# A hybrid decoder block in fp32: every second transposed-form weight unit takes its low halves from adding DMAs issued by GpSimd

## The chip, the core and the metric

The kernel runs on one core of a Trainium2 chip. The metric is the device time of one execution in microseconds (us). Two executions of the kernel before took 1184.29 and 1184.67 us, median 1184.48 us. The profile shown below is one further execution of the same program; its span, from its first to its last instruction, is 1182.7 us.

The engines are named as the profile names them: PE is the matrix engine (PEld its weight loads), DVE the vector engine, ACT the scalar engine, POOL is GpSimd, SP the engine that here only issues DMAs. A "q" behind an engine's name is its instruction queue.

## The reference, cut to what matters

One decoder layer on 256 tokens of width 2048, everything in float32:

```python
h = rms_norm(x, g_pre[l])
proj = h @ w_in[l]                      # 2048 x 17,936, split into 14 parts
y_a = pool_mixer(a_val, a_gate, ...)    # causal pooling, width 1024
y_b = swa_mixer(sq, sk, sv, s_gate)     # windowed attention, 12 heads of 128
y_c = gla_mixer(cq, ck, cv, c_lr, c_gate, ...)   # gated linear attention, 4 heads
y_m = mem_attn(mq, m_gate, mem, ...)    # attention into 256 memory tokens
gates = jax.nn.sigmoid(g_logits + b_merge[l])
merged = sum of gates[b] * (y_b @ w_br_b)        # four branches
x = x + rms_norm(merged @ w_out[l], g_post[l])
```

Nearly all of the arithmetic is in the products with the weights, which are read once each; the DMAs move 230 MB in all.

## The kernel before, in words

**Split products.** A float32 product is made from rounded halves. Every weight tile `raw` is split into `hi`, which is `raw` rounded to the matrix engine's reduced format (fp32r), and `lo = raw - hi`, rounded likewise; the activations are split in the same way. A product is then hi·hi + hi·lo + lo·hi. `split_w` (L110 to L115) does it for weights, up to 1024 columns at a time: L113 is the rounding copy on ACT, L114 the subtraction on DVE. Such a piece of 128 x 1024 is called a half here, since two of them make one loaded unit of 128 x 2048 (1 MB).

**Two forms of a product.** `a_block` (L117) keeps the activations stationary and streams the weights. `b_unit` (L146) is the transposed form: the weights are stationary and the activations stream. One unit makes 128 output columns for all 256 tokens: 16 k-steps, each one matmul with `hi` against both halves of the activations (512 columns, L156) and one with `lo` against their high half (256 columns, L157). There are 72 such units: the queries and keys of the window attention (`sq`, `sk`, 24 units, names such as `sk01` for head 0, group 1), its gate (`sg`, 4), the memory keys (`km`, 4), the memory queries and gates (`mq`, `mg`, 8), the linear attention's queries and keys (`cq`, `ck`, 8) and gate (`cg`, 8), the pooling values and gates (`av`, `ag`, 16). Everything else goes through `a_block`: the values, the merge gates (`g...`), the branch projections (`b...`) and the output (`o0` to `o4`).

**Buffers.** A unit is loaded by SP (`load_raw`, L107) into one of 3 `raw` buffers. There are 5 `hi` and 5 `lo` buffers, each for one half. So the split of a half can begin when the matmuls that read the half five places earlier are done, four halves before its own turn on PE. An SP load waits until the `raw` buffer is free again, and the loads behind it wait with it.

**After a unit**, ACT copies the second half of the accumulator out (`...s`, L161), DVE adds the first half to it (L162) and scales it; a gate also goes through a tanh on ACT (L306).

**Background work.** The attention heads, the linear attention and the pooling are generators in a queue. `pull(1)` (L68) runs one step of the first generator; `b_unit` calls it between its two halves (L159) and at its end (L164), `a_block` after every or every second half. Each step's instructions stand in the engines' streams at that point, with one `yield` between what is made and what uses it.

**Order.** Each engine runs its own instructions strictly in the order in which the built program has them. That order is set when the program is built, and differs in places from the order of the code. An instruction that waits holds up all that stand behind it on its engine.

Of the kernel before, what the change touches and what calls it, by code (L numbers as in the profile page):

```python
# [9 lines left out]
R = mybir.dt.float32r  # L10
AF = mybir.ActivationFunctionType
ALU = mybir.AluOpType
AX = mybir.AxisListType

P = 128
# [14 lines left out]
NB_HILO = 5  # L30
# [7 lines left out]
def kernel(ctx, tc, ins, out):  # L38
    nc = tc.nc
    ten, vec, act, pool, sync = nc.tensor, nc.vector, nc.scalar, nc.gpsimd, nc.sync  # L40

    cst = ctx.enter_context(tc.tile_pool(name="cst", bufs=1))
    wp = ctx.enter_context(tc.tile_pool(name="wp", bufs=1))
# [15 lines left out]
    def acc(name, shape):  # L59
        return ps.tile(shape, F32, tag="acc", bufs=4, name=name)  # L60
# [1 line left out]
    def tiny(name, shape, bufs=4):  # L62
        return big.tile(shape, F32, tag="tiny", bufs=bufs, name=name)

# [1 line left out]
    queue = []  # L66

    def pull(n):  # L68
        while n > 0 and queue:
            try:  # L70
                next(queue[0][1])
                n -= 1
            except StopIteration:
                queue.pop(0)
# [5 lines left out]
            except StopIteration:  # L80
                queue.pop(0)

# [1 line left out]
    vecs = cst.tile([P, 52], F32, name="vecs")  # L84
    act.dma_start(vecs[:], ins["vecs"])
    ones = cst.tile([P, P], F32, name="ones")
# [11 lines left out]
    half = cst.tile([P, 2], F32, name="half")  # L98
    pool.memset(half[:], -0.5)

# [1 line left out]
    raw_count = [0]  # L102

    def load_raw(src, n):
        raw = wp.tile([P, 2048], F32, tag="raw", bufs=NB_RAW, name=f"raw{raw_count[0]}")
        raw_count[0] += 1
        sync.dma_start(raw[:, :n], src[:, :n])  # L107
        return raw

    def split_w(raw_ap, n, name):  # L110
        hi = wp.tile([P, 1024], R, tag="hi", bufs=NB_HILO, name=name + "h")
        lo = wp.tile([P, 1024], R, tag="lo", bufs=NB_HILO, name=name + "l")
        act.activation(hi[:, :n], raw_ap, AF.Copy)  # L113
        vec.tensor_tensor(lo[:, :n], raw_ap, hi[:, :n].bitcast(F32), op=ALU.subtract)  # L114
        return hi, lo  # L115

    def a_block(name, units, stat, nw, evac, load=None, per_split=None):  # L117
        """out[token, column]: activations stationary, weights moving."""
        accs = [acc(f"{name}a{t}", [P, 512]) for t in range(2)]
        nk = 4 * len(units)  # L120
        for u, src in enumerate(units):
            raw = load_raw(src, 4 * nw) if load is None else load(u, src)
            nk_s = max(1, 1024 // nw) if per_split is None else per_split(u)
            for hf in range(4 // nk_s):
                hi, lo = split_w(raw[:, hf * nk_s * nw : (hf + 1) * nk_s * nw], nk_s * nw, f"{name}{u}{hf}")
                for kk in range(nk_s):
                    k = 4 * u + nk_s * hf + kk
                    ws = slice(kk * nw, (kk + 1) * nw)
                    for t in range(2):
                        sh, sl = stat(k)  # L130
                        ts = slice(t * P, (t + 1) * P)
                        o = accs[t][:, :nw]
                        ten.matmul(o, lhsT=sh[:, ts], rhs=hi[:, ws], start=(k == 0), stop=False)  # L133
                        ten.matmul(o, lhsT=sh[:, ts], rhs=lo[:, ws], start=False, stop=False)  # L134
                        ten.matmul(o, lhsT=sl[:, ts], rhs=hi[:, ws], start=False, stop=(k == nk - 1))  # L135
                if hf % 2 == 0:
                    pull(1)
            pull(1)

        def finish():  # L140
            for t in range(2):
                evac(t, accs[t][:, :nw])

        return finish

    def b_unit(name, src, mov, evac):  # L146
        """out[column, token]: weights stationary, activations moving."""
        a = acc(f"{name}a", [P, 512])
        raw = load_raw(src, 2048)
        for hf in range(2):  # L150
            hi, lo = split_w(raw[:, hf * 1024 : (hf + 1) * 1024], 1024, f"{name}{hf}")
            for kk in range(8):
                k = 8 * hf + kk
                ws = slice(kk * P, (kk + 1) * P)
                mh, _ = mov(k)
                ten.matmul(a[:], lhsT=hi[:, ws], rhs=mov.both(k), start=(k == 0), stop=False)  # L156
                ten.matmul(a[:, :T], lhsT=lo[:, ws], rhs=mh, start=False, stop=(k == KT - 1))  # L157
            if hf == 0:
                pull(1)  # L159
        both = c2(f"{name}s", [P, T])  # L160
        act.activation(both[:], a[:, T:], AF.Copy)  # L161
        vec.tensor_tensor(both[:], a[:, :T], both[:], op=ALU.add)  # L162
        evac(both[:])
        pull(1)  # L164

# [1 line left out]
    def make_T(name, srcT, g):  # L167
        hl = [e8(f"{name}hl{i}", [P, 4, 2, T], R) for i in range(4)]

# [25 lines left out]
        return chunk, at  # L195

    def make_rstd(name, src):
        """1/rms of each token: a column per token tile, and along the free axis for all partitions."""
        ssq = cst.tile([P, 2, 2], F32, name=f"{name}ssq")
        mean = cst.tile([P, 2], F32, name=f"{name}mean")  # L200
        col = cst.tile([P, 2], F32, name=f"{name}col")
        row = cst.tile([P, T], F32, name=f"{name}row")

        def gen():
            for t in range(2):
                for c in range(2):
                    xt = c4(f"{name}x{t}{c}", [P, D // 2])
                    sync.dma_start(xt[:], src[t][:, c * (D // 2) : (c + 1) * (D // 2)])
                    act.activation(xt[:], xt[:], AF.Square, accum_out=ssq[:, t, c : c + 1])
                    yield  # L210
            vec.tensor_tensor(mean[:], ssq[:, :, 0], ssq[:, :, 1], op=ALU.add)
            vec.tensor_scalar(mean[:], mean[:], 1.0 / D, EPS, op0=ALU.mult, op1=ALU.add)
            pool.tensor_tensor(col[:], mean[:], half[:], op=ALU.pow)
            yield
            pr = sm(f"{name}pr", [P, T])
            dg = c2(f"{name}dg", [P, T])
            for t in range(2):
                vec.tensor_scalar(
                    dg[:, t * P : (t + 1) * P], ident[:], col[:, t : t + 1], None, op0=ALU.mult
                )  # L220
            yield
            yield
            ten.matmul(pr[:], lhsT=ones[:], rhs=dg[:], start=True, stop=True)
            vec.tensor_copy(row[:], pr[:])
            yield

        return col, row, gen
# [7 lines left out]
        for _ in gen:  # L235
            pass

    # ================= window attention: values =================
    sv = [c4(f"sv{g}", [P, 2, 512]) for g in range(3)]

    def sv_evac(j):
# [42 lines left out]
    queue.append(("memprep", mem_prep()))  # L284
    a_block("sv2", [ins["w_sv"][2, u] for u in range(4)], h_at, 512, sv_evac(2))()

    # constants that the branches need later
    big_cst = cst.tile([P, 1344], F32, name="big_cst")
    sync.dma_start(big_cst[:], ins["consts"])
    dist0 = big_cst[:, 0:384].rearrange("p (g j) -> p g j", g=3)  # L290
# [6 lines left out]
    vec.tensor_scalar(p_scale, p_scale, 0.5, None, op0=ALU.mult)  # L297

    def silu2_evac(dst):
        """2 * silu of the normalised product."""  # L300

        def evac(a):
            xg = c2("xg", [P, T])
            vec.tensor_tensor(xg[:], a, row[:], op=ALU.mult)  # L304
            th = c2("th", [P, T])
            act.activation(th[:], xg[:], AF.Tanh, scale=0.5)  # L306
            vec.scalar_tensor_tensor(dst, th[:], 1.0, xg[:], op0=ALU.add, op1=ALU.mult)

        return evac
# [11 lines left out]
        act.activation(hi, full, AF.Copy)  # L321
        vec.tensor_tensor(lo, full, hi.bitcast(F32), op=ALU.subtract)  # L322

    # ================= window attention =================
    yb = e8("yb", [P, 2, 4, T], R)
    sgate = c4("sgate", [P, 4, T])

# [53 lines left out]
        queue.append(("swa", swa_head(hh, q3, k3)))  # L381
    drain("memprep")

    # ================= attention into the memory =================
    ym = e8("ym", [P, 2, 4, T], R)
    km = c4("km", [P, 4, T])
    mq = c4("mq", [P, 4, T])
# [43 lines left out]
        b_unit(f"mg{h}", ins["w_mg"][h], h_at, silu2_evac(mgate[:, h, :]))  # L431
        queue.append(("mem", mem_head(h)))

    # ================= gates and branch projections =================
    merged = [e8(f"merged{t}", [P, D]) for t in range(2)]
    started = [False] * 4

# [27 lines left out]

    merge("swa", 1, lambda k: (yb[:, 0, k, :], yb[:, 1, k, :]), 4)

    # ================= gated linear attention =================
    gq = c4("gq", [P, 4, T])
    gk = c4("gk", [P, 4, T])  # L470
    cv = e8("cv", [P, 2, 1024])
# [14 lines left out]
    def gla():  # L486
# [11 lines left out]
        z = c4("z", [P, 4, T])  # L498
        for hp in range(2):
            pz = sm(f"pz{hp}", [P, 2, T])  # L500
            for i in range(2):
                h = 2 * hp + i
                ten.matmul(pz[:, i, :], lhsT=walpha[:, h * P : (h + 1) * P], rhs=lrT[:], start=True, stop=True)
            for i in range(2):
                h = 2 * hp + i
                vec.tensor_scalar(z[:, h, :], pz[:, i, :], b_alpha[:, h : h + 1], None, op0=ALU.add)
        yield
        # log_sigmoid(z) = min(z, 0) - log(1 + exp(-|z|))
        e = c4("e", [P, 4, T])
        act.activation(e[:], z[:], AF.Abs)  # L510
        act.activation(e[:], e[:], AF.Exp, scale=-1.0)
# [26 lines left out]
        for h in range(4):  # L538
# [61 lines left out]
            for vt in range(2):  # L600
                f = 2 * h + vt
# [13 lines left out]
    for j in range(3):  # L615
        c0, n = CV_BLOCKS[j]
# [4 lines left out]

    merge("mem", 3, lambda k: (ym[:, 0, k, :], ym[:, 1, k, :]), 4)

    # ================= causal pooling =================
    PAD = 16
    ya = [e8(f"ya{i}", [P, 8, T], R) for i in range(2)]
    agate = {}
# [78 lines left out]

    merge("pool", 0, lambda k: (ya[0][:, k, :], ya[1][:, k, :]), 8, after=transpose_block)

    # ================= output projection, norm, residual =================
    gpost = e8("gpost", [P, D])  # L710
    xres = [e8(f"xres{t}", [P, D]) for t in range(2)]
    yg = [e8(f"yg{t}", [P, D]) for t in range(2)]
# [28 lines left out]
    for u in range(4):  # L741
        raw = load_raw(ins["w_last"][1, u], 1024)
        last.append(split_w(raw[:, :1024], 1024, f"o4{u}"))
    for t in range(2):
        ts = slice(t * P, (t + 1) * P)
        a = acc(f"o4a{t}", [P, 512])[:, :256]
        for k in range(KT):
            hi, lo = last[k // 4]
# [16 lines left out]
def _layout(x, mem, g_pre, g_post, g_mem, w_in, b_merge, w_pool, pool_scale, w_alpha, b_alpha,  # L765
# [47 lines left out]
    }  # L813
    for j, (c0, n) in enumerate(CV_BLOCKS):
        d[f"w_cv{j}"] = units_a(np.ascontiguousarray(cvlr[:, c0 : c0 + n]), n)[0]
    # constants of the shapes: distances to the keys that each window sees, masks, counts
    i = np.arange(T)[:, None]
    j = np.arange(T)[None, :]
    dist = []
# [5 lines left out]
    a, b = np.arange(P)[:, None], np.arange(P)[None, :]  # L825
# [23 lines left out]
```

## Time and profile before

| | before |
|---|---|
| device time, median of 2 | 1184.48 us (1184.29 to 1184.67) |
| profiled execution, span | 1182.7 us |
| median less span | 1.8 us |
| PE busy | 1172.6 us, 99% |
| DVE busy | 715.9 us, 61% |
| ACT busy | 555.3 us, 47% |
| POOL busy | 13.8 us, 1% (36 instructions) |
| DMA moved | 230.44 MB, mean 195 GB/s |
| granted PE clock | 0.998 |

How to read it. The device time is a little longer than the span because it holds what lies before the first and after the last instruction. A row of grouped instructions gives the line of the kernel, the engine, the operation, what is written and read, the count, the busy time with the mean of one in ns, and the idle time before them with what ended it. A row of one tile gives minimum, median and maximum duration in ns and the first and last start in us. A row of the timeline gives start and duration in us. A row of the stretches gives the stretch, its length, the busy time of each engine with instruction counts, the granted clock, the mean busy share of the 16 DMA engines and GB/s. A row of the DMA issues gives the size of one and the median time from issue to landing.

### The profile page before, as it was taken

The numbers are of one execution on the slowest core, as the hardware profiler recorded it, in microseconds if no ns is written. First come the engines' busy times: TensorE is split into PE (matmuls) and PEld (weight loads), VectorE is DVE, ScalarE is ACT, GpSimd is POOL, SyncE is SP. The second block draws the span as 40 slices with busy tenths as digits, with TensorE's granted clock in tenths as the row PEclk, the third lists the DMA queues.
The fourth block names the chain that finished last, engine by engine and source line by source line (L and its number), as shares of the span: only waits on it lengthen the run. The fifth ranks groups of instructions, "written<-read, shape, count | busy, mean of one in ns | idle before, by whom it ended". The sixth has DMA issues, their size and how long they took to land.

```text
span 1182.7 us, 15065 instructions
## 1 busy us (share of the span) xinstructions
PE 1172.6 (99%) x6014; PEld 1001.8 (85%) x6014; DVE 715.9 (61%) x943; ACT 555.3 (47%) x734; POOL 13.8 (1%) x36
## 2 busy tenths in 40 slices
PE   9999999999999999999999999999999999999997
PEld 7888888888888888899888888888888888888887
DVE  6656665664665555545856666777655555656454
ACT  7656444444554444345644444454444444444441
POOL 0000000000000000000000000000000000000000
PEclk9999999999999999999999999999999999999999
DMA  9867544544445555356444455555555555556642
GB/s 354 324 226 260 178 147 175 178 148 174 178 169 192 200 199 201 133 185 221 178 163 176 156 184 199 179 186 194 214 193 205 204 189 205 193 187 241 257 145 105
DMA packets 38838, 230.44 MB, mean 195 GB/s; under 512 B 4448, under 2 KB 4832, under 8 KB 14832
## 3 DMA queue, kind: packets, MB, share of 16 engines
q1 hardware_dynamic: 38048, 228.28, 54.5%
q10 hardware_dynamic: 720, 1.21, 0.3%
q8 instruction: 47, 0.77, 0.3%
q14 instruction: 23, 0.19, 0.0%
HBM read 227.37 MB, written 2.10 MB: 194 GB/s over the span
## 4 chain that ended last, share of the span: by engine, by line
PE 98%; issue 0%; DMA 0%; DVE 0%; ACT 0%; SPq 0%; DVEq 0%; POOLq 0%; POOL 0%
PE sp L341 1%; PE gmem0a L133 1%; PE gmem2a L133 1%; PE gmem1a L133 1%; PE gswa0a L135 1%; PE gmem2a L135 1%; PE gswa0a L133 1%; PE gmem0a L135 1%; PE gmem1a L135 1%; PE vma L135 1%; PE gmem2a L134 1%; PE gmem0a L134 1%; PE gpool1a L135 1%; PE o0a L135 1%; PE gmem1a L134 1%; PE vma L133 1%
## 5 line engine op out<-in xcount | busy, mean ns | idle before, releaser
L306 ACT ACTIVATE th<-xg 128x256 f32<-128x256 f32 x24 | 9.9, 411 | 18.1 <-DVE xg L304 18.1
L344 DVE SCALAR_TENSOR_TENSOR s<-big_cst,sp 128x128 f32<-128x128 f32 (+1 forms) x24 | 7.3, 349 | 3.5 <-PE sp L341 3.5
L341 PE MATMUL sp<-k,q 128*128 128x128 f32 (+1 forms) x48 | 9.1, 326 | 0.0
L349 ACT ACTIVATE s<-s,st 128x384 f32<-128x384 f32 (+1 forms) x8 | 6.2, 775 | 4.8 <-DVE st L348 4.8
L341 PEld LDWEIGHTS sp<-k,q 128*128 128x128 f32 x48 | 7.3, 190 | 0.8
L578 POOL TENSOR_TENSOR sq<-sq 128x256 f32<-128x256 f32 x4 | 3.4, 854 | 384.5 <-ACT sq L577 360.4
L179 ACT ACTIVATE xhl<-xr,vecs 128x256 fp32r<-128x256 f32 x16 | 6.9, 499 | 1.9 <-DMA xr<-in_xT 1.2
L704 ACT ACTIVATE mTh<-mtp 128x512 fp32r<-128x512 f32 x8 | 4.3, 596 | 6.5 <-PE mtp L702 6.5
L180 DVE SCALAR_TENSOR_TENSOR xhl<-xr,vecs,xhl 128x256 fp32r<-128x256 f32 x16 | 6.8, 482 | 0.7 <-ACT xhl L179 0.6
L367 PE MATMUL po<-pt,sv 128*128 128x256 f32 x24 | 7.2, 380 | 0.0
L179 ACT ACTIVATE mhl<-mr,vecs 128x256 fp32r<-128x256 f32 x16 | 7.0, 495 | 0.0
L180 DVE SCALAR_TENSOR_TENSOR mhl<-mr,vecs,mhl 128x256 fp32r<-128x256 f32 x16 | 6.9, 479 | 0.0
L759 DVE SCALAR_TENSOR_TENSOR yg<-yg,opart,xres 128x640 f32<-128x640 f32 (+2 forms) x8 | 5.5, 748 | 1.3 <-POOL opart L756 1.3
L348 DVE TENSOR_REDUCE st<-s 128x1 f32<-128x384 f32 (+1 forms) x8 | 6.0, 748 | 0.1
L726 ACT ACTIVATE oj<-o4a 128x256 f32<-128x256 f32 x2 | 0.8, 383 | 10.6 <-PE o4a L753 10.6
L362 ACT ACTIVATE pt<-tp 128x384 f32<-128x384 f32 x12 | 5.7, 477 | 0.0
L705 DVE SCALAR_TENSOR_TENSOR mTl<-mtp,mTh 128x512 fp32r<-128x512 f32 x8 | 5.2, 686 | 0.7 <-ACT mTh L704 0.4
L322 DVE TENSOR_TENSOR sqh<-sq,sqh 128x256 fp32r<-128x256 f32 x4 | 1.7, 424 | 5.9 <-ACT sqh L321 5.9
L456 DVE TENSOR_TENSOR merged<-merged,gmem 128x512 f32<-128x512 f32 x8 | 5.1, 684 | 0.0
L456 DVE TENSOR_TENSOR merged<-merged,ggla 128x512 f32<-128x512 f32 x8 | 5.1, 684 | 0.0
L456 DVE TENSOR_TENSOR merged<-merged,gpool 128x512 f32<-128x512 f32 x8 | 5.1, 684 | 0.0
L368 PEld LDWEIGHTS po<-pt,sv 128*128 128x128 f32 x24 | 4.6, 190 | 0.6
(3495 smaller groups left out, 4397.0 us busy)
## 6 DMA issues: line engine op xcount, KB each, us to landing
raw<-in_w_g SPq DMA_DIRECT2D x64, 1024.0 KB, 4.8
raw<-in_w_sqk SPq DMA_DIRECT2D x24, 1024.0 KB, 4.9
raw<-in_w_out SPq DMA_DIRECT2D x12, 1024.0 KB, 4.8
raw<-in_w_sv SPq DMA_DIRECT2D x8, 1024.0 KB, 7.7
raw<-in_w_cqk SPq DMA_DIRECT2D x8, 1024.0 KB, 4.8
raw<-in_w_cg SPq DMA_DIRECT2D x8, 1024.0 KB, 4.9
raw<-in_w_av SPq DMA_DIRECT2D x8, 1024.0 KB, 4.8
raw<-in_w_ag SPq DMA_DIRECT2D x8, 1024.0 KB, 4.9
```

Of the source, the lines that this page charges most:

```text
L133: ten.matmul(o, lhsT=sh[:, ts], rhs=hi[:, ws], start=(k == 0), stop=False)
L134: ten.matmul(o, lhsT=sh[:, ts], rhs=lo[:, ws], start=False, stop=False)
L135: ten.matmul(o, lhsT=sl[:, ts], rhs=hi[:, ws], start=False, stop=(k == nk - 1))
L179: act.activation(h, rawx[:, i, :], AF.Copy, scale=g[:, k : k + 1])
L180: vec.scalar_tensor_tensor(l, rawx[:, i, :], g[:, k : k + 1], h.bitcast(F32), op0=ALU.mult, op1=ALU.subtract)
L306: act.activation(th[:], xg[:], AF.Tanh, scale=0.5)
L341: ten.matmul(parts[g], lhsT=q3[:, g, it * P : (it + 1) * P], rhs=k3[:, g, :nj], start=True, stop=True)
L344: vec.scalar_tensor_tensor(s[:, g, :], dist[:, g, :], SLOPES[g * 4 + hh], parts[g], op0=ALU.mult, op1=ALU.add)
L348: vec.tensor_reduce(st[:, 0:1], s[:], axis=AX.XY, op=ALU.max, negate=True)
L349: act.activation(s[:], s[:], AF.Exp, bias=st[:, 0:1], accum_out=st[:, 1:2])
L367: ten.matmul(po[:], lhsT=sv[g][:, 0, vs], rhs=pt[g][:, 0:T], start=(g == 0), stop=False)
L456: vec.tensor_tensor(merged[t][:, js], merged[t][:, js], gates[t][:], op=ALU.add)
```

## The change

A second way to split a half, `split_w_dma`, is used by every second call of `b_unit`, 36 of the 72, for both halves. In it ACT writes the negated rounding of `raw` into the `lo` tile; a DMA issued from GpSimd's queue then adds the unrounded weights to what stands in the tile, so that `raw - hi` is left there. For the first half the DMA reads the `raw` tile, for the second half it reads the weights once more from HBM. ACT then makes `hi` as before. In both kinds of unit the two halves are now split in the code ahead of the first matmul, and the step of background work stays between the halves' matmuls. Nothing else is changed but comments.

```diff
+    def split_w_dma(raw_ap, src, n, name):
+        hi = wp.tile([P, 1024], R, tag="hi", bufs=NB_HILO, name=name + "h")
+        lo = wp.tile([P, 1024], R, tag="lo", bufs=NB_HILO, name=name + "l")
+        act.activation(lo[:, :n], raw_ap, AF.Copy, scale=-1.0)
+        pool.dma_start(lo[:, :n], src, accum_op=ALU.add)
+        act.activation(hi[:, :n], raw_ap, AF.Copy)
+        return hi, lo
+
+    b_count = [0]
...
     def b_unit(name, src, mov, evac):
         a = acc(f"{name}a", [P, 512])
         raw = load_raw(src, 2048)
+        by_dma = b_count[0] % 2 == 1
+        b_count[0] += 1
+        parts = []
         for hf in range(2):
-            hi, lo = split_w(raw[:, hf * 1024 : (hf + 1) * 1024], 1024, f"{name}{hf}")
+            cs = slice(hf * 1024, (hf + 1) * 1024)
+            if by_dma:
+                parts.append(split_w_dma(raw[:, cs], src[:, cs] if hf else raw[:, cs], 1024, f"{name}{hf}"))
+            else:
+                parts.append(split_w(raw[:, cs], 1024, f"{name}{hf}"))
+        for hf in range(2):
+            hi, lo = parts[hf]
             for kk in range(8):
```

In the changed kernel the three lines of `split_w_dma` are L121 (negated copy), L122 (the DMA) and L123 (`hi`); the lines from `b_unit` on stand 20 further down, so L161 before is L181 after.

PE's instructions stand in the same order in both programs. POOL has 72 instructions more than before, ACT 72 more and DVE 72 fewer; on SP four loads stand a few places later than before. Three places where the order moves follow, each before and after.

ACT, where the linear attention's background work runs between the gate units `cg`. Rows are line, operation, what is written from what; `cg50` and `cg51` are the two halves of unit `cg5`, ending in `h` or `l` for `hi` or `lo`; `cg3s` is the copy that follows the last matmul of `cg3`. Before:

```order
L161 ACTIVATE cg2s<-cg2a 128x256
L529 ACTIVATE kd<-kd 128x1024
L530 ACTIVATE ep<-bc 128x1024
L113 ACTIVATE cg50h<-raw_4952 128x1024
L113 ACTIVATE cg51h<-raw_4952 128x1024
L306 ACTIVATE th<-xg 128x256
L161 ACTIVATE cg3s<-cg3a 128x256
L113 ACTIVATE cg60h<-raw_5019 128x1024
```

After:

```order
L181 ACTIVATE cg2s<-cg2a 128x256
L549 ACTIVATE kd<-kd 128x1024
L550 ACTIVATE ep<-bc 128x1024
L123 ACTIVATE cg50h<-raw_5004 128x1024
L123 ACTIVATE cg51h<-raw_5004 128x1024
L326 ACTIVATE th<-xg 128x256
L181 ACTIVATE cg3s<-cg3a 128x256
L121 ACTIVATE cg50l<-raw_5004 128x1024
L121 ACTIVATE cg51l<-raw_5004 128x1024
L113 ACTIVATE cg60h<-raw_5073 128x1024
```

The two negated copies of `cg5` now stand behind `cg3s`, which waits for the end of `cg3` on PE; one unit, `cg4`, lies between that and `cg5`.

ACT, at the first transposed-form units, while the memory tokens are being prepared (`mhl` is their split, `sq00s` the copy after unit `sq00`). Before:

```order
L113 ACTIVATE sq010h<-raw_770 128x1024
L179 ACTIVATE mhl_101<-mr_688,vecs 128x256 x4
L113 ACTIVATE sq011h<-raw_770 128x1024
L113 ACTIVATE sk010h<-raw_823 128x1024
L161 ACTIVATE sq00s<-sq00a 128x256
L113 ACTIVATE sk011h<-raw_823 128x1024
L113 ACTIVATE sq020h<-raw_874 128x1024
```

After:

```order
L113 ACTIVATE sq010h<-raw_772 128x1024
L113 ACTIVATE sq011h<-raw_772 128x1024
L123 ACTIVATE sk010h<-raw_825 128x1024
L199 ACTIVATE mhl_101<-mr_692,vecs 128x256
L181 ACTIVATE sq00s<-sq00a 128x256
L199 ACTIVATE mhl_101<-mr_692,vecs 128x256 x3
L121 ACTIVATE sk010l<-raw_825 128x1024
L121 ACTIVATE sk011l<-raw_825 128x1024
L123 ACTIVATE sk011h<-raw_825 128x1024
```

The negated copies of `sk01` stand behind the end of `sq00` and three of the memory tokens' splits, and two units (`sk00`, `sq01`) lie between the end of `sq00` and `sk01`.

POOL, at the end of the `cg` units (`sq` and `ms` are sums and roots of the linear attention's output norm). Before:

```order
L488 MEMSET scan_m 128x1024
L489 MEMSET scan_m 128x16
L578 TENSOR_TENSOR sq_5015<-sq_5015 128x256
L590 TENSOR_TENSOR ms_5077<-ms_5077,half 128x2
L578 TENSOR_TENSOR sq_5263<-sq_5263 128x256
```

After:

```order
L122 DMA cg30l<-raw_4879 128x1024
L122 DMA cg31l<-in_w_cg 128x1024
L122 DMA cg50l<-raw_5004 128x1024
L122 DMA cg51l<-in_w_cg 128x1024
L122 DMA cg70l<-raw_5135 128x1024
L122 DMA cg71l<-in_w_cg 128x1024
L598 TENSOR_TENSOR sq_5069<-sq_5069 128x256
L610 TENSOR_TENSOR ms_5131<-ms_5131,half 128x2
```

The first sum of the norm now stands behind the DMAs of `cg7`, each of which waits on POOL's queue for its negated copy on ACT.

## Prediction

> **What bounds the kernel now.** I read the page's busy times and slices first, then the chain of waits.
>
> ```profile
> span 1182.7 us, 15065 instructions
> PE 1172.6 (99%) x6014; PEld 1001.8 (85%) x6014; DVE 715.9 (61%) x943; ACT 555.3 (47%) x734; POOL 13.8 (1%) x36
> PEclk9999999999999999999999999999999999999999
> PE 98%; issue 0%; DMA 0%; DVE 0%; ACT 0%; SPq 0%; DVEq 0%; POOLq 0%; POOL 0%
> ```
> Then the list of what PE waited for, which has three entries:
> ```profile
> PE cold L92 <- POOL ones L87: 1.0, 1, 1.0
> PE sv0a L133 <- ACT sv000h L113: 0.9, 1, 0.9
> PE sv0a L133 <- ACT sv001h L113: 0.4, 1, 0.4
> ```
> PE is busy for all but 1182.7 - 1172.6 = 10.1 us, at full clock; the chain is PE; its listed waits add up to 2.3 us and lie at the very start, ahead of every transposed-form unit. So DVE, at 61%, is waited for nowhere that the change touches. The question is only whether PE stays fed.
>
> **The change part by part.** One half's matmuls, one split, and the copy after a unit, by tile and from the timeline:
> ```profile
> L156 PE MATMUL sq10a<-xhl,sq100h x8: 395/398/403, 112.6 to 115.1; 128*128 128x512 f32 x8
> L156 PE MATMUL sq10a<-xhl,sq101h x8: 395/398/403, 115.5 to 117.9; 128*128 128x512 f32 x8
> L113 ACT ACTIVATE ag310h<-raw x1: 1060/1060/1060, 804.3 to 804.3; 128x1024 fp32r<-128x1024 f32 x1
> L114 DVE TENSOR_TENSOR ag310l<-raw,ag310h x1: 1226/1226/1226, 805.4 to 805.4; 128x1024 fp32r<-128x1024 f32 x1
> 79.76 0.37 ACT L161 ACTIVATE sq00s<-sq00a 128x256 f32<-128x256 f32 x1
> ```
> *Removed:* 72 subtractions of 1.23 us, 88 us of DVE. None is on the path, so this alone is worth nothing. *Added on ACT:* 72 copies of 1.06 us, 76 us; ACT goes from 555 to 632 us (53%), which PE's time covers on average, though not at every moment (below). *Moved:* PE's order is the same word for word; that both splits are now emitted ahead of the matmuls costs nothing by itself, since the five half buffers bound how early a split can start.
>
> *The adding DMA* replaces a subtraction that ended 1.06 + 1.23 = 2.3 us after its half's split began. No row shows such a DMA. What it must do is known from the code: for 512 KB written, two times 512 KB are read, the weights and the tile itself. The nearest rows are plain loads, SP's issue of one, and what POOL itself runs:
> ```profile
> raw<-in_w_sqk SPq DMA_DIRECT2D x24, 1024.0 KB, 4.9
> raw<-in_w_last SPq DMA_DIRECT2D x8, 512.0 KB, 3.4
> msx<-in_mem SPq DMA_DIRECT2D x4, 512.0 KB, 7.8
> L107 SPq DMA_DIRECT2D raw<-in_w_sqk x24: 327/328/340, 50.7 to 207.9; - x24
> 101.26 0.70 POOL L213 TENSOR_TENSOR mscol<-msmean,half 128x2 f32<-128x2 f32 x1 [60.37 <-DVE msmean L212]
> 679.28 1.20 POOL L578 TENSOR_TENSOR sq<-sq 128x256 f32<-128x256 f32 x1 [24.17 <-issue]
> ```
> Twice the size adds 1.5 us, so 1.9 us are fixed. Low end: it lands like a 512 KB load, 3.4 us. My value: two reads make it like the 1 MB load, 4.9 us. High end: a third pass, 1.5 us more, or a crowded queue, in which a 512 KB load took 7.8 us. For POOL's issue I take 0.7 us, its smallest arithmetic, between SP's 0.3 and POOL's longest sum, 1.2. A 1 MB load in flight on the same engines can hold it up by its own 2 x 1.5 = 3.0 us. So from issue to landing: about 4 us at the low end, 5.6 to 8.6 us at my value, 10 and more at the high end.
>
> [...]
>
> *The time there is.* A half takes PE 115.5 - 112.6 = 2.9 us. Its buffers come free four halves ahead, 11.5 us; the negated copy, with another copy and an evacuation ahead of it on ACT, takes 1.06 + 1.06 + 0.37 = 2.5 us of that. Some 9 us are left for 8.6: ordinary units hold, barely. ACT's and POOL's new order makes shorter windows:
> ```profile
> 559.00:576.00 17.00, 15.10 (x19) 1.00 0.17 63
> 573.93 0.36 ACT L161 ACTIVATE cg3s<-cg3a 128x256 f32<-128x256 f32 x1
> L157 PE MATMUL cg5a<-xhl,cg50l x8: 274/279/280, 580.9 to 583.3; 128*128 128x256 f32 x8
> 91.73 1.30 ACT L179 ACTIVATE mhl<-mr,vecs 128x256 fp32r<-128x256 f32 x3
> L157 PE MATMUL sk01a<-xhl,sk010l x8: 277/281/284, 90.3 to 92.7; 128*128 128x256 f32 x8
> L113 ACT ACTIVATE ag110h<-raw x1: 1062/1062/1062, 756.2 to 756.2; 128x1024 fp32r<-128x1024 f32 x1
> L157 PE MATMUL ag11a<-xhl,ag110l x8: 278/281/284, 766.3 to 768.7; 128*128 128x256 f32 x8
> L113 ACT ACTIVATE ag210h<-raw x1: 1063/1063/1063, 780.2 to 780.2; 128x1024 fp32r<-128x1024 f32 x1
> L157 PE MATMUL ag21a<-xhl,ag210l x8: 277/281/284, 790.3 to 792.8; 128*128 128x256 f32 x8
> L157 PE MATMUL ag31a<-xhl,ag310l x8: 277/281/284, 812.9 to 815.4; 128*128 128x256 f32 x8
> 591.14 0.74 POOL L578 TENSOR_TENSOR sq<-sq 128x256 f32<-128x256 f32 x1 [311.77 <-ACT sq L577]
> L587 PE MATMUL pq<-ones_r,sqh x16: 166/250/263, 594.0 to 683.5; 128*128 128x2 f32 x16
> ```
> - `cg5`: ACT, busy 15.1 of the 17.0 us up to there, gets `cg3`'s two negated copies (2.1 us) on top, of which idle time takes perhaps 1; then `cg3s` (to 574.3 before) and 1.06 us for `cg50l`: ready about 576.5, wanted by PE at 580.9, 4 us later. Late by 2 to 4.5 us: 4 us with the second half.
> - `sk01`: 79.8 + 0.4 + 1.3 (three of the memory tokens' splits) + 1.06 = 82.5, wanted at 90.3: 7.8 us, where a 512 KB load lands in 7.8; with the second read, 9.3, and POOL's 0.7 it is 2 us late, the second half behind it as much. With smaller delays in `sk02` and `sq10`: 6 us.
> - `ag11`: 756.2 + 2.1 (`hi`, then the negated copy) = 758.3 to 766.3, 8.0 us; `ag21`: 782.3 to 790.3, 8.0 us; `ag31`: 806.4 to 812.9, 6.5 us. Late by up to 2 us each, and in sum as much again for second halves and for the DVE units whose splits ACT then starts late: 9 us.
> - The norm behind `cg7`: POOL's sum starts at 591.1 and PE reads what comes of it at 594.0 with nothing to spare. ACT, which makes its input, gets there 2 us later for `cg7`'s two copies: 2 us.
> - The other 30 units: 0.1 us each, 3 us.
>
> Queues passed: behind a waiting DMA on POOL stand only other adding DMAs, that norm, and small memsets. On SP, `raw` before came free 2.3 us after its second half's split began; now it waits for the first half's adding DMA, at worst 2.5 + 8.6 us after a start one half (2.9 us) earlier, so 8.2 us, 6 later. The next split in that buffer begins five halves (14.4 us) after, and a load takes 4.9: 14.4 - 4.9 - 2.3 = 7 us cover the 6. Without that cover each unit would lose the excess.
>
> Sum: 4 + 6 + 9 + 2 + 3 = 24 us. Profile 1182.7 + 24 + 1.8 (median 1184.48 less span) = 1208.5, say **1209 us**, just over 2% slower; one microsecond of landing more or less in the dozen late halves makes its own range 1197 to 1221.
>
> **The rivals.** For both, the stretches of transposed-form units; the DMA share stands next to last:
> ```profile
> q1 hardware_dynamic: 38048, 228.28, 54.5%
> 70.00:110.00 40.00, 40.00 (x224) 34.56 (x223) 24.92 (x37) 24.85 (x39) 0.70 (x1) 1.00 0.75 274
> 110.00:240.00 130.00, 130.00 (x756) 114.09 (x755) 82.08 (x130) 59.23 (x88) 0.00 (x0) 1.00 0.47 164
> 240.00:330.00 90.00, 90.00 (x491) 77.77 (x490) 53.21 (x78) 42.84 (x65) 1.08 (x2) 1.00 0.50 176
> 455.00:500.00 45.00, 45.00 (x253) 38.97 (x252) 25.10 (x32) 18.07 (x24) 0.00 (x0) 1.00 0.48 167
> 545.00:590.00 45.00, 45.00 (x267) 39.40 (x266) 35.58 (x51) 29.68 (x41) 0.00 (x0) 1.00 0.49 178
> 715.00:820.00 105.00, 105.00 (x594) 91.20 (x594) 76.56 (x118) 49.71 (x69) 0.62 (x5) 1.00 0.52 188
> ```
> *Hidden after all.* If an adding DMA lands in 4 us, or in 5.6 without queueing, only `cg5` (up to 2 us) and the norm (2 us) are late: 1184.5 + 4 = 1188 us. For it: the DMA engines are half idle in five of six stretches. It decides below about 6 us. This is the case that is not slower.
>
> *The DMA engines become the bound.* SP's queue spent 0.545 x 1182.7 / 228.28 = 2.82 us of all engines per MB, so 512 KB (0.524 MB) cost 1.48 us a pass. The stretches get 8, 20, 12, 8, 8 and 16 adding DMAs. At two passes (2.96 us) their DMA time becomes 54 of 40, 120 of 130, 81 of 90, 45 of 45, 46 of 45 and 102 of 105 us: full, but only the first overflows, and partly into the room of the next. At three passes (4.44 us) it is 66, 150, 98, 57, 58 and 126 us, an overflow of 26 + 20 + 8 + 12 + 13 + 21 = 100 us: 1284 us. It decides from just above two passes. [...]
>
> *Faster.* All of PE's idle time is 10 us, part of it before the first unit: at best 1175 us, less than can be told. That the subtractions don't leave DVE is out: it has 72 rows fewer.
>
> **How the numbers follow.** About 2% (24 us: below 1160.8, above 1208.2) is what a measurement of this kernel can tell from no change. The forecast has 0.50, of it 0.28 above that line and 0.22 below; hidden 0.27, of it 0.01 for a true gain of a few microseconds; DMA-bound, everything above 1221, 0.22; faster by over 2%, by something that I don't see, 0.01. So faster 0.01, same 0.49, slower 0.50. The range, 1185 to 1280, goes down to the hidden case with hardly a wait and up to nearly three passes, and leaves out less than 0.1 at each end.
>
> **What would show it.** Right: PE waits before `cg50l`, `sk010l`, `ag110l`, `ag210l`, `ag310l` and `pq`, some 24 us in all; adding DMAs that land in 5 to 9 us; a DMA share near 0.9 in these stretches. Landing under 5 us and hardly a wait: the first rival. Waits in nearly every second unit and a share of 1: the second. Wrong altogether: slower matmuls, or PE waiting for `hi`.

## The result, and the profile after

The changed kernel takes 1221.06 us, the median of two runs (1218.81 to 1223.31), against 1184.48 us before: 1.031 times as long, with a 95% interval of 1.026 to 1.035. The page of the profile after, its busy times, slices, queues and chain:

```profile
span 1221.5 us, 15266 instructions
PE 1186.5 (97%) x6014; PEld 1010.7 (83%) x6014; DVE 632.9 (52%) x871; ACT 621.9 (51%) x806; POOL 77.2 (6%) x108
PEclk9999999999999999999899999988999999999999
...
q0 software_dynamic: 10368, 37.75, 16.7%
PE 30%; DMA 2%; issue 1%; ACT 0%; DVE 0%; DVEq 0%; POOLq 0%; POOL 0%; SPq 0%; ACTq 0%
```

DVE gave up 83 us and ACT took 67 us, and still the span grew by 1221.5 - 1182.7 = 38.8 us. PE is still the bound, but it is now made to wait. (The chain's shares no longer add up to the span, so it does not tell the cause.) PE's idle time went from 10.1 to 35.0 us, 24.9 us more. The same 6014 matmuls were also busy 13.9 us longer, and three slices of the clock line show an 8. These two terms make up the 38.8 us.

What PE waits for, after (engine, tile and line, what it waited for; us in total, times, longest):

```profile
PE ag31a L177 <- DMA ag310l<-raw: 4.7, 1, 4.7
PE cg5a L177 <- DMA cg50l<-raw: 4.2, 1, 4.2
PE ag20a L176 <- ACT ag200h L113: 3.9, 1, 3.9
PE sk01a L177 <- DMA sk010l<-raw: 3.7, 1, 3.7
...
PE ag10a L176 <- ACT ag100h L113: 1.5, 1, 1.5
PE ag11a L177 <- DMA ag110l<-raw: 1.2, 1, 1.2
...
PE pq L607 <- DVE sqh L342: 0.9, 1, 0.9
...
PE ag10a L177 <- DVE ag100l L114: 0.8, 1, 0.8
PE sk02a L177 <- DMA sk021l<-in_w_sqk: 0.6, 1, 0.6
PE av21a L177 <- DMA av210l<-raw: 0.6, 1, 0.6
PE ag21a L177 <- DMA ag210l<-raw: 0.6, 1, 0.6
PE ag20a L177 <- DVE ag200l L114: 0.5, 1, 0.5
PE av31a L177 <- DMA av310l<-raw: 0.4, 1, 0.4
PE ag21a L177 <- DMA ag211l<-in_w_ag: 0.2, 1, 0.2
```

The left-out rows are the three at the very start, which the kernel before has too. The others add up to 23.8 us: 4.2 at `cg5`, 4.3 at `sk01` and `sk02`, 0.9 at the norm, and 14.4 in the pooling units `av` and `ag`, of which 6.7 us wait for ACT or DVE, not for an adding DMA.

The second term shows in stretches cut at `cg5` (columns as in the prediction's rows of stretches; the granted clock is the third number from the end), and in one row by tile:

```profile
593.90:598.00 4.10, 4.10 (x13) 3.52 (x14) 0.42 (x1) 0.77 (x2) 0.67 (x1) 0.50 1.01 234
598.00:602.00 4.00, 4.00 (x28) 3.58 (x26) 0.00 (x0) 2.00 (x2) 0.87 (x1) 1.00 1.03 301
L176 PE MATMUL cg5a<-xhl,cg50h x8: 393/628/628, 589.2 to 598.1; 128*128 128x512 f32 x8
```

Behind the wait of 4.2 us PE runs at a granted clock of 0.50, and does 13 matmuls in the time in which it then does 28. The matmul of 395 ns takes 628 ns. There are five such stretches between the first units and the pooling: 3.41 us at 96.3 (behind `sk01`), 6.83 at 591.2 (`cg5`), 3.41 at 778.9 (`ag10`), 6.83 at 809.6 (`ag20`) and 6.83 at 847.2 (`ag31`). They last 27.3 us, of which PE waits 6.5. The other 20.8 us of work at half rate cost 10.4 us of the 13.9; a 3.41 us stretch at 10.9 us, behind the waits at the start, costs up to 1.7 more, and 1.8 us are not placed. The stretch at 10.9 us stands in none of the other profiles, so it says little of the change. The second execution after, 1218.81 us, had a mean granted clock of 0.989 against 0.985 in this profile: how much half clock there is differs from one execution to the next.

Five of the six stretches of transposed-form units after, for comparison with those of the prediction (DMA share next to last):

```profile
70.00:110.00 40.00, 36.35 (x193) 31.16 (x192) 13.83 (x25) 28.13 (x41) 6.10 (x7) 0.96 0.98 291
110.00:240.00 130.00, 129.40 (x751) 113.23 (x750) 57.99 (x109) 80.09 (x110) 18.17 (x21) 1.00 0.91 259
240.00:330.00 90.00, 90.00 (x492) 77.84 (x491) 39.05 (x62) 50.65 (x69) 9.50 (x11) 1.00 0.80 229
455.00:500.00 45.00, 45.00 (x243) 38.61 (x242) 16.56 (x22) 26.82 (x31) 7.57 (x10) 1.00 0.88 250
...
715.00:820.00 105.00, 96.59 (x490) 81.40 (x489) 47.95 (x77) 51.98 (x65) 10.89 (x17) 0.95 0.73 210
```

In the second, third and fourth, 40 adding DMAs run beside loads at a DMA share of 0.80 to 0.91, and PE waits 0.6 us. A DMA share this high does not by itself stop this kernel.

### The profile page after: what moved, and what is told of

It reads as the page before. It is cut to its first block, busy times and chain, and to the rows that moved or that the text cites. A ratio compares the mean times of both kernels' runs of the same rounds, so it can differ in the third digit from the quotient of the medians.

```text
span 1221.5 us, 15266 instructions
## 1 busy us (share of the span) xinstructions
PE 1186.5 (97%) x6014; PEld 1010.7 (83%) x6014; DVE 632.9 (52%) x871; ACT 621.9 (51%) x806; POOL 77.2 (6%) x108
## 3 DMA queue, kind: packets, MB, share of 16 engines
q1 hardware_dynamic: 38048, 228.28, 52.2%
q0 software_dynamic: 10368, 37.75, 16.7%
## 5 line engine op out<-in xcount | busy, mean ns | idle before, releaser
L176 PE MATMUL ag20a<-xhl,ag200h 128*128 128x512 f32 x8 | 5.2, 649 | 3.9 <-ACT ag200h L113 3.9
L122 POOL DMA_DIRECT2D cq10l<-raw x1 | 0.9, 859 | 120.7 <-DVE gswa L467 120.7
L177 PE MATMUL ag31a<-xhl,ag310l 128*128 128x256 f32 x8 | 3.3, 411 | 4.7 <-DMA ag310l<-raw 4.7
L177 PE MATMUL cg5a<-xhl,cg50l 128*128 128x256 f32 x8 | 3.3, 410 | 4.2 <-DMA cg50l<-raw 4.2
L177 PEld LDWEIGHTS ag31a<-xhl,ag310l 128*128 128x128 f32 x8 | 2.5, 307 | 5.0 <-DMA ag310l<-raw 5.0
L177 PE MATMUL sk01a<-xhl,sk010l 128*128 128x256 f32 x8 | 3.0, 380 | 3.7 <-DMA sk010l<-raw 3.7
L176 PEld LDWEIGHTS ag20a<-xhl,ag200h 128*128 128x128 f32 x8 | 2.6, 325 | 4.8 <-ACT ag200h L113 4.2
L177 PEld LDWEIGHTS cg5a<-xhl,cg50l 128*128 128x128 f32 x8 | 2.5, 307 | 4.5 <-DMA cg50l<-raw 4.5
```

## The experiments

The theory after the result: the loss is the waits at a few units whose negated copies come late on ACT, plus a half clock behind the longer waits. The rivals: the adding DMAs load the DMA engines everywhere, ACT's extra copies are the cost, or the half clock comes from something else than the waits.

**A plain copy in place of the adding DMA.** This kernel leaves the subtraction out: `lo` holds the weights themselves. Order, sizes and queues stay.

```diff
-        pool.dma_start(lo[:, :n], src, accum_op=ALU.add)
+        pool.dma_start(lo[:, :n], src)
```

> The adding DMAs become plain copying DMAs from the same source into the same tile (the low halves are then the weights themselves; the subtraction is left out). Every engine's order stays word for word. Theory (an adding DMA makes two passes over its bytes on the shared DMA engines, so it lands late): GpSimd's queue takes about half its 16.7% share, median landing falls from 6.0 to about 4 us, waits remain at cg5 alone, 1186 to 1194 us. Rival (ACT's added copies and the new order on ACT and POOL make the waits, or GpSimd's slow issue does): waits stay, 1212 us or more.

Measured: 1193.13 us (1192.37 to 1195.09), 1.007 times before (1.006 to 1.009). Its queue, PE's longest waits in it, and the landing of its 72 copies beside that of the adding DMAs (the last row, from after):

```profile
q0 software_dynamic: 10368, 37.75, 9.4%
PE ag21a L177 <- DMA ag210l<-raw: 1.8, 1, 1.8
PE sk01a L177 <- DMA sk010l<-raw: 1.2, 1, 1.2
PE cg5a L177 <- DMA cg50l<-raw: 0.7, 1, 0.7
DMA to landing us min/median/max: 2.9/4.9/9.3
```
```profile
DMA to landing us min/median/max: 4.5/6.0/11.0
```

The time came as the theory expected, though the copies land in 4.9 us at the median and not in 4, and the waits that are left lie at several places and not at `cg5` alone. The adding itself is worth 28 of the 36.6 us. It also gives the price that no row of before had: 0.167 x 1221.5 / 72 = 2.83 us of all 16 engines for an adding DMA, 0.094 x 1191.6 / 72 = 1.56 us for a copy of the same 512 KB, a ratio of 1.82.

**ACT's copies stay, DVE adds.** No DMA on POOL; DVE does one operation per half, as before the change.

```diff
-        pool.dma_start(lo[:, :n], src, accum_op=ALU.add)
+        vec.tensor_tensor(lo[:, :n], lo[:, :n].bitcast(F32), raw_ap, op=ALU.add)
```

> ACT keeps its negated copies, but DVE adds the weights onto them, with no adding DMA. Theory: without the DMAs nothing lands late, 1184 to 1188 us, though ACT has its 76 us more. Rival (ACT's load is what starves PE): 1200 us or more.

Measured: 1184.99 us, 1.000 times before (0.999 to 1.001). ACT's 72 more copies cost nothing by themselves. Nor does ACT's new order at `cg5` and in the pooling units, which this kernel has too but for a few places; at `sk01` its order differs from that of the changed kernel, so there the order is not tested.

**DVE splits in nine late units, adding DMAs in the other 27.**

```diff
+LATE = ("sk01", "sk02", "cg5", "av11", "ag11", "av21", "ag21", "av31", "ag31")
...
-        by_dma = b_count[0] % 2 == 1
+        by_dma = b_count[0] % 2 == 1 and name not in LATE
```

> The changed kernel in which the nine units around which PE waited (sk01, sk02, cg5, av11, ag11, av21, ag21, av31, ag31) are split by DVE as before; 27 units keep their adding DMAs. Theory (the cost lies in the few short windows; the other adding DMAs are hidden): 1185 to 1190 us. Rival (the adding DMAs cost something everywhere, through the shared DMA engines): about 27/36 of the loss stays, 1212 us.

Measured: 1185.94 us, 1.001 times before (1.000 to 1.002). The landing of its 54 adding DMAs, and PE's waits for them:

```profile
DMA to landing us min/median/max: 4.5/7.7/11.0
PE sq10a L178 <- DMA sq100l<-raw: 0.4, 1, 0.4
PE sq30a L178 <- DMA sq300l<-raw: 0.4, 1, 0.4
```

So 27 of the 36 units hide their adding DMAs, even with a median landing of 7.7 us. The whole loss hangs on the nine, which holds against the DMA engines as the bound. Which part of it is the nine units' DMAs and which their copies and order on ACT, this run does not tell.

**Work in the place of the waits.** 78 throw-away matmuls, about 0.23 us apart, ahead of the five longest waits.

```diff
+FILL = {"sk01": 15, "cg5": 17, "ag10": 9, "ag20": 18, "ag31": 19}
...
+        for _ in range(FILL.get(name, 0)):
+            ten.matmul(a[:], lhsT=mov(0)[0][:, :P], rhs=mov.both(0), start=True, stop=True)
```

> The changed kernel with 78 matmuls of 0.23 us whose result is thrown away, put ahead of the five units that wait longest (15, 17, 9, 18 and 19 ahead of sk01, cg5, ag10, ag20 and ag31), so that PE works through about 18 us in which it waited. Theory (each wait is followed by some microseconds at half clock, 15 us in all): the waits are replaced one for one, the half clock goes, 1205 to 1210 us. Rival (the half clock comes from something else, or the waits only move behind the fill): 1221 us or more.

Measured: 1220.25 us (1218.58 to 1223.43), 1.030 times before (1.028 to 1.032); the expected 1205 to 1210 was missed. Its PE busy time and the longest of its waits:

```profile
PE 1197.4 (98%) x6092; PEld 1020.2 (84%) x6092; DVE 632.6 (52%) x871; ACT 620.8 (51%) x806; POOL 77.2 (6%) x108
PE ag11a L180 <- DMA ag110l<-raw: 2.6, 1, 2.6
PE pq L610 <- ACT sqh L344: 1.6, 1, 1.6
```

The fill is 78 x 0.23 = 17.9 us, so 1197.4 - 1172.6 - 17.9 = 6.9 us of half clock are left of 13.9. That half of the test agrees with the theory. But new waits came up behind the fill, at `pq`, `ag11` and others, and two of these places were again followed by 6.83 and 3.41 us at half clock. PE was idle for 19.4 us, 9.3 more than before, so the rival that the waits only move behind the fill held for a part of them. The run does not separate the two terms as cleanly as was meant.

**Stops of PE put into the kernel before.** Ahead of six blocks at full clock (`ggla2`, `bgla2`, `ggla3`, `bgla3`, `o1`, `o2`) PE waits for a two-column copy by ACT, followed by 4, 0 or 1 small sums on POOL.

```diff
+        if name in GAP:
+            link = tiny(f"{name}gap", [P, 2])
+            act.activation(link[:], last_acc[0][1][:, 0:2], AF.Copy)
+            for i in range(CHAIN):
+                pool.tensor_tensor(link[:], link[:], half[:], op=ALU.add)
+            for t in range(2):
+                ten.matmul(accs[t][:, 0:2], lhsT=ident[:], rhs=link[:], start=True, stop=True)
```

> The kernel before, with a chain ACT, four small POOL sums, PE put between six pairs of streamed blocks (ggla2 to bgla3, o1, o2), so that PE stands idle six times for about 4 us. Theory (an idle PE of that length is followed by 3.4 to 6.8 us at half clock, a loss of 1.7 to 3.4 us): six waits of 4 us and 10 to 20 us more, 1219 to 1230 us. Rival (no loss behind a wait): 1208 us, at full clock.

> As the six waits of 4 us in the kernel before, but with the chain over ACT alone, so that PE stands idle six times for about 1 us. Theory (the clock is halved only behind waits of some length): about 6 us of waits and no half clock, 1190 to 1192 us. Rival (any wait halves it): 10 to 20 us more, 1200 us or more.

> As the six waits in the kernel before, with one small POOL sum in the chain, for waits of about 2 to 3 us, between the 1.3 to 2.2 us that left the clock whole and the 3.3 to 3.9 us that halved it for 3.4 us each time. If the clock is halved behind waits of this length too: about 14 us of waits, 4 of restarts and 10 of half clock, 1211 to 1214 us. If not: 1201 to 1204 us.

| sums | stops, us each | time, us, and ratio | over before, us | six stops, us | rest, us |
|---|---|---|---|---|---|
| 4 | 3.3 to 3.9 | 1221.17, 1.031 (1.029 to 1.032) | 36.3 | 21.6 | 14.7 |
| 1 | 1.6 to 3.0 | 1214.00, 1.023 (1.021 to 1.026) | 28.9 | 14.2 | 14.7 |
| 0 | 1.3 to 2.2 | 1199.65, 1.013 (1.011 to 1.014) | 14.8 | 10.6 | 4.2 |

The stops and the clock are those of the profiled executions. With no sums the clock stays at 1.00 and a stop costs its length and 0.7 us; the time missed the expected 1190 to 1192 us, because the stops were longer than 1 us and because of these 0.7 us, whose cause stays open. The other two times lie in their expected ranges. With one or four sums every stop is followed by 3.41 us at 0.50 (one by 6.83), and the rest is 10.5 us larger: 1.75 us for each of six, half of 3.41. So a wait of this kind in an undisturbed place costs its length and, when the half clock follows, about 1.7 us on top. Yet the length of a stop alone does not seem to decide. The same stop, ahead of `bgla2`, with no sum and with one, as PE's timeline has it (idle time in brackets), and stretches of 3.41 us around it:

```profile
912.67 0.61 PE L131 MATMUL bgla2a<-bgla2gap,ident 128*128 128x2 f32 x4 [2.24 <-ACT bgla2gap L127]
908.22:911.63 3.41, 2.21 (x10) 1.50 (x8) 2.62 (x4) 1.75 (x3) 0.00 (x0) 1.00 0.37 108
911.63:915.05 3.42, 2.38 (x12) 2.06 (x13) 1.15 (x1) 0.99 (x3) 0.00 (x0) 1.00 0.88 344
```
```profile
913.88:917.29 3.41, 1.49 (x9) 1.32 (x10) 1.59 (x2) 1.59 (x4) 0.19 (x1) 1.00 0.92 330
917.29:920.70 3.41, 3.41 (x10) 2.67 (x9) 0.00 (x0) 0.00 (x0) 0.00 (x0) 0.51 0.14 55
```

The stop of 2.24 us lies across two stretches, 1.2 us in one and 1.0 in the other, and nothing follows: the clock is 1.00 in both, and it stays there until PE's work ends. In the run with one sum 1.9 us lie in one stretch, and the next is at half clock; with one sum, stops of 1.60 us that lay within one stretch were followed by it as well. The four executions with one sum took from 1209.99 us, at a mean granted clock of 0.992, to 1215.46 us, at 0.988, so the same stops are not always followed by as much half clock.

**Three short stops, close together or apart.** The same instructions in two orders: three stops ahead of each of the six blocks, with 1 or with 8 throw-away matmuls between them, 24 in all.

```diff
+STOPS = (8, 1, 1)      # or (8, 8, 8)
...
+            for fill in STOPS:
+                for _ in range(fill):
+                    ten.matmul(accs[0][:, :256], lhsT=ident[:], rhs=big_cst[:, :256], start=True, stop=True)
+                link = tiny(f"{name}gap", [P, 2])
+                act.activation(link[:], accs[0][:, 0:2], AF.Copy)
+                ten.matmul(accs[0][:, 0:2], lhsT=ident[:], rhs=link[:], start=True, stop=True)
```

> This is the kernel before with three short stops of TensorE ahead of each of six blocks (ggla2, bgla2, ggla3, bgla3, o1, o2). A stop is a copy of two columns of the last throw-away product by ScalarE, which TensorE waits for; such a stop took 1.25 us in the run with six single stops where ScalarE was free. 24 throw-away matmuls stand ahead of each block; here 8, 1 and 1 of them lie ahead of the three stops, and 14 behind: the three stops stand within some 5 us. Theory (the half clock comes when TensorE idles over about 1.6 us in all within one window of a 3.41 us grid that runs on by itself): every one of the six groups is followed by at least 3.41 us at 0.50, though each stop by itself is shorter than 1.5 us; the time is 6 to 12 us above that of the run with the stops spread. Rival (what counts is the length of one stop): no half clock, and the same time as the run with the stops spread, within 2 us.

> The same instructions in the same number as in the run with three stops close together, but 8 of the 24 throw-away matmuls lie ahead of each of the three stops, so that about 3 us of work part them. Theory (idle time within one window of a 3.41 us grid): hardly any half clock, at most where a single stop gets longer than 1.6 us because ScalarE is busy; 6 to 12 us below the run with the stops close together. Rival (the length of one stop): the same time as that run within 2 us.

Measured: 1252.57 and 1252.55 us, each 1.057 times before. The two are equal, but this speaks for no theory, since there were no stops. PE's timeline of the first:

```profile
887.38 3.61 PE L126 MATMUL ggla2a<-big_cst,ident 128*128 128x256 f32 x16
890.64 0.58 PE L144 MATMUL ggla2a<-ggla200h,xhl 128*128 128x512 f32 x1
...
891.29 0.34 PE L129 MATMUL ggla2a<-ggla2gap,ident 128*128 128x2 f32 x2
```

The built program had put two matmuls of the block's other accumulator where each stop was to be, and they covered ACT's copy.

**The pooling weights' loads on GpSimd's queue.** In after, ACT stands at `wpl0h`, `wpl1h` and `wpl2h` for the loads `wpr`, which SP issues behind loads that wait for a `raw` buffer. For `wpl1h`, SP's wait and the issue of its load, and ACT's copy with the wait ahead of it, in after and then in before:

```profile
SPq L107 <- DMA av210l<-raw: 11.3, 1, 11.3
800.61 0.45 SPq L676 DMA_DIRECT2D wpr<-in_w_pool  x1
808.17 0.63 ACT L113 ACTIVATE wpl1h<-wpr 128x512 fp32r<-128x512 f32 x1 [8.36 <-DMA wpr<-in_w_pool]
```
```profile
771.66 0.42 SPq L656 DMA_DIRECT2D wpr<-in_w_pool  x1
776.65 0.63 ACT L113 ACTIVATE wpl1h<-wpr 128x512 fp32r<-128x512 f32 x1 [2.96 <-DMA wpr<-in_w_pool]
```

ACT's turn comes at 799.8 us in after and at 773.7 in before. SP issued the load 0.8 us behind that in after and 2.0 us ahead of it in before, which is 2.8 us of the 5.4 that the wait grew by. The other 2.6 are the load's own landing, 7.5 us against 5.0.

The experiment issues these loads from POOL:

```diff
-        sync.dma_start(wr[:], ins["w_pool"][g])
+        pool.dma_start(wr[:], ins["w_pool"][g])
```

> The changed kernel with the four loads of the pooling mix weights (wpr, 256 KB) issued from GpSimd's queue and not from SP's. Theory (wpr comes late because it stands on SP behind loads that wait until an adding DMA has read raw; ACT stands at its split and so ag10 and ag20 wait for their hi): the waits at ag10 and ag20, 6.7 us, and the half clock behind them, 5 us, go: 1208 to 1212 us. Rival (the DMA engines are simply full there): the waits stay, 1219 to 1223 us.

Measured: 1211.54 us (1209.45 to 1213.22), 1.022 times before (1.021 to 1.024), 9.5 us under after. ACT's waits for `wpr` went from 5.1, 8.4 and 8.7 us to 5.1, 7.0 and 2.0. Where they fell most, behind `wpl2h`, the 4.7 us before `ag310l` are gone, though that DMA lands as in after, in 4.9 us against 4.8, and ACT's order there is the same: `ag31` was late because ACT was. The waits for `ag100h` and `ag200h` are gone too, but there the edit also moved ACT's order: `wpl0h`, `wpl1h` and the two copies now stand ahead of `av10s` and `av20s`, and no longer behind the end of those units. So at these two places the load's queue is not shown to be the cause. The first three loads of `wpr` land no sooner from POOL's queue, in 6.9 to 8.8 us against 7.3 to 8.0. In place of these waits `ag21` waits longer:

```profile
PE ag21a L177 <- DMA ag210l<-raw: 5.0, 1, 5.0
```

In sum the waits of the pooling units fall from 14.4 to 8.0 us. The time was as expected, the cure only partial.

**Both halves from HBM, and both from `raw`.**

```diff
-                parts.append(split_w_dma(raw[:, cs], src[:, cs] if hf else raw[:, cs], 1024, f"{name}{hf}"))
+                parts.append(split_w_dma(raw[:, cs], src[:, cs], 1024, f"{name}{hf}"))
```

> The changed kernel with both adding DMAs of a unit reading the weights from HBM, none from raw, so raw comes free when ACT has read it. Theory (SP held up by the adding DMAs that read raw is one part of the loss): SP no longer waits for adding DMAs, ag10 and ag20 wait less, the landing is about as before: 1205 to 1216 us. Rival (reading again from HBM is the costly part): 18.9 MB more from HBM, more waits, 1225 us or more.

> The changed kernel with both adding DMAs of a unit reading the weights from raw, none from HBM. If collisions of SP's loads with the second adding DMA make the landing (as when raw was freed earlier, and landing rose), raw freed later keeps the load away from both: second halves land about 1 us sooner than the 6.2 us of the changed kernel, but the loads start later and ACT waits for raw in places: 1210 to 1222 us. Rival (late raw is the larger harm): many waits for hi, 1235 us or more.

Measured: 1228.00 us for HBM (1.037; 1.036 to 1.039), and 1224.90 us for `raw` (1.035; 1.031 to 1.038). The queue's share and the landing, HBM first, then `raw`; the third row is of `raw` too, SP's wait for a second half:

```profile
q0 software_dynamic: 10368, 37.75, 16.7%
DMA to landing us min/median/max: 5.2/8.5/14.6
```
```profile
q0 software_dynamic: 10368, 37.75, 15.9%
DMA to landing us min/median/max: 5.0/8.9/13.1
SPq L107 <- DMA km31l<-raw: 13.5, 1, 13.5
```

Neither came out as the theory expected. With HBM the time lies in the rival's range (1225 us or more), but not for its reason: the time on the engines is the same or a little less, so the source doesn't set the price. The median landing rose from 6.0 us to 8.5 and 8.9. The median of all 72 is a poor measure, though: three runs with unchanged adding DMAs (nine units, fill, `wpr`) have 7.6 to 7.7, because the units from `sq10` to `sg3` land in 9.0 to 9.4 us there and in 5.7 in after; why, stays open. From `mg0` to `ck3`, where those runs agree with after (5.4 to 5.7 us), it is 8.2 us with HBM and 8.6 with `raw`, so there the rise is real. In both runs ACT's order moved at `av10s` and `av20s` as with `wpr`. With HBM, SP no longer waits for the first half's DMA, and its next loads are issued earlier, beside the adding DMAs; that the landing rises for this reason is argued from the timelines and not shown. For `raw` SP waits up to 13.5 us, and why the landing rises there stays open.

## Why the prediction was right, and where its sum fell short

The forecast, just over 2% slower by PE waiting for late adding DMAs at a few units, came true: 1221 us against 1209, at the upper end of its own range (1197 to 1221). Of the 38.8 us that the span grew by, 16.2 are PE waiting directly for an adding DMA, by the list of waits. Its steps:

- *Removed subtractions, worth nothing; ACT's 76 us covered.* Right, and ACT's busy time rose by 67 us only. The second is shown by DVE adding in the DMA's place (1184.99 us), the first by the nine units put back, where DVE is 64 us below before and the time is unchanged.
- *The adding DMA as two reads, landing in 5.6 to 8.6 us.* Right in the main: 6.0 us at the median, at `cg50l` 8.8 and at `sk010l` 8.2, though single ones take up to 11.0. The engine time, forecast at 2.96 us, is 2.83. That an adding DMA costs like two reads was an estimate, since no row of before shows one; the run with the plain copy shows 2.83 us against 1.56, a ratio of 1.82, and a landing of 6.0 us at the median against 4.9. POOL's issue was put at 0.7 us and is 0.86.
- *`cg5`, 4 us; `sk01` and its followers, 6; the norm, 2.* Measured 4.2, 4.3 and 0.9. The working at `cg5` holds in detail. PE's first matmul of the unit starts at 589.2 us, and POOL issues `cg50l`'s DMA 4.2 us ahead of that, where the forecast had about 4:

```profile
585.03 0.86 POOL L122 DMA_DIRECT2D cg50l<-raw  x1 [12.91 <-ACT cg50l L121]
```

- *`ag11`, `ag21`, `ag31` and followers, 9 us.* Measured 14.4 us in the pooling units. This step failed in its cause. It took ACT's times there from before and added the copies; but 10.1 us of it, `ag31` and the waits for `ag100h` and `ag200h`, lie right behind ACT standing at the pooling weights. For the 4.7 us at `ag31` the run with `wpr` on POOL's queue shows this; for the other 5.4 it is read from the timeline.
- *SP's later release of `raw`, covered by 7 us.* Right for the next `raw` load of ordinary units, as the 27 units show. But that step looked only at those loads; `wpr` is queued behind them on the same queue, and ACT waits for it. That was overlooked, and so was that a load itself lands later beside the adding DMAs: at `wpl1h` each is about half of the longer wait.
- *The other 30 units, 3 us.* Next to nothing; too high.
- *The sum, 24 us.* The waits are 23.8 us. That they match is luck: the excess in the pooling units and the shortfalls elsewhere cancel. The sum had no term for the half clock behind a wait, and that is most of the 13.9 us by which PE's busy time grew. "Wrong altogether: slower matmuls", it said of what would disprove it; the matmuls did get slower, but behind the waits and because of them, as the stops put into the kernel before show. It named PE waiting for `hi` as well, and PE did, 5.4 us at `ag10` and `ag20`.
- *The rivals.* "Hidden after all" holds for 27 units and fails at nine. "DMA-bound" does not hold: 2.83 us is two passes and not three, and three stretches at a share of 0.80 to 0.91 lose 0.6 us. This rival, like the 3.0 us by which a load was to hold up an adding DMA, took it that adding DMAs and loads run on the same engines, which no row of before could show. After, the page counts `q0`'s 16.7% and `q1`'s 52.2% as shares of the same 16 engines, and the loads `raw<-in_w_sqk` land in 6.2 us at the median against 4.9 before, which fits; how long one load holds up one adding DMA no run shows. The DMA share, forecast near 0.9, is 0.73 to 0.98.

No version ran below the time before. PE was busy for 99% of it, and the two that equal it do so by taking the waits away.

## What to carry to other kernels

PE, busy for 99% of the time, lost more than the length of its waits: 24.9 us of them took 38.8. When a buffer is to be released later, follow every load queued behind the one that waits, who waits for that load, and how much later it lands beside the new DMAs, not only the next use of the buffer. Work moved off an engine that nobody waits for gains nothing, and where the replacement's latency nearly fills the lead, the units with the shortest lead decide; leaving out nine of 36 gave the whole loss back.

## What the runs showed of the hardware that was not expected

PE's clock falls to 0.50 behind waits of only 1.6 to 4.7 us, for 3.41 or 6.83 us. Within each profile all these stretches begin and end on a grid of 3.41 us. In after it is 843.09 us, 247 times 3.413, from the start of the first at 10.93 us to the end of the last that PE works in, at 854.02, and the full-clock stretches between them last 81.92, 491.52, 180.91, 27.31 and 30.72 us, which is 24, 144, 53, 8 and 9 times 3.413; with one sum, the full-clock stretches between the stops last 23.89, 10.24, 23.89, 167.25 and 23.89 us, which is 7, 3, 7, 49 and 7 times 3.413. Laid on this grid, in the 14 profiles, from 10 us after the start to the step with PE's last matmul, every one of the 34 full-clock steps in which PE idled 1.8 us or more was followed by half clock; none of the 41 with 0.7 to 1.5 us was; between 1.5 and 1.8 it was 5 of 11. In after the five followed by it had 1.51, 2.00, 2.05, 3.17 and 3.41 us of idle time, the longest of the others 1.17. So it seems to be the idle time within one step that counts, about half of it, and by this estimate where a stop falls on the grid decides for stops between about 1.6 and 3.4 us. This is read from the traces and argued; the pair of runs meant to test it had no stops.

The landing of an adding DMA spread from 4.5 to 11.0 us in after, and the same units landed in 5.7 us in one run and in 9.0 to 9.4 in others, while the mean time on the engines stayed at 2.7 to 2.8 us for each. What sets the landing is not shown.
